# A two-layer diffusion-transformer step: the conditioning parts in another order, some of them placed at stage borders, and a first MLP group of eight tiles

## The chip, the cores and the metric

The kernel runs on one NeuronCore of a Trainium2 chip. The metric is the device time of one execution in microseconds (us); lower is better. The time before is the median of three runs.

## The reference, cut to what matters

Two streams of 128 tokens each (context and latent) with 2048 channels pass through two layers. Layer 0 mixes tokens with differential attention and a two-way RWKV-7 scan; layer 1 is a Conformer convolution module. A gated ConvFFN (the MLP) follows each of them. All is in float32.

```python
def adaln(cvec, w, b):                      # w_ada: (2 layers, 2048, 6*2048)
    return (silu(cvec) @ w + b)[:, None, :]

for l in range(2):
    sh1, sc1, g1, sh2, sc2, g2 = split(adaln(c, w_ada[l], b_ada[l]), 6)   # once for c, once for c_ctx
    h = rmsnorm(x, norm_g[l, 0]) * (1 + sc1) + sh1
    m = ab_mixer(h, ...) if l == 0 else conformer_conv(h, ...)
    x = x + g1 * m
    h = rmsnorm(x, norm_g[l, 1]) * (1 + sc2) + sh2
    x = x + g2 * conv_ffn(h, w_up[l], w_ffn_dw[l], w_down[l])
y = rmsnorm(x, final_norm_g)

def conformer_conv(h, ...):
    u = h @ w_pw1                           # 2048 -> 4096
    u = u[..., :2048] * sigmoid(u[..., 2048:])
    u = dwconv(u, w_dw) + b_dw              # 31 taps
    return silu(layernorm(u)) @ w_pw2

def conv_ffn(h, ...):                       # D_FF = 5504 = 43 tiles of 128
    u = dwconv(h @ w_up, w_ffn_dw)          # 3 taps
    gate, val = split(u, 2)
    return (silu(gate) * val) @ w_down
```

The twelve vectors `sh1 ... g2` of two layers are the conditioning. Each is a product of two vectors (`c` and `c_ctx`, through SiLU) with a 2048 x 2048 piece of `w_ada`, so 16.8 MB of weights are read for each of them and almost nothing is computed.

## The kernel before, in words

Activations lie with channels on the 128 partitions and 256 tokens (two streams of 128) on the free axis; 2048 channels are 16 tiles, counted by `kt`. Matrix products go through `gemm` (line 235). A plan is a list of groups; a group is a set of output tiles that accumulate in PSUM together. For each group `gemm` walks over all `kt`, and for each `kt` and each output tile TensorE issues three matmuls of 128x128 by 128x256: high part of the weight by high part of the activation (line 252), high by low (254), low by high (255). So a group of four tiles costs 12 matmuls in each `kt`, one of eight tiles 24. In the last group of some products (`tail=4`) the last four `kt` are issued tile by tile (lines 268 to 270), with an optional call `between()` ahead of them.

The weights come from HBM in pieces of 128 x 1024 floats (512 KB) into a tile `raw` (`emit_load`, line 180). ScalarE copies the high part to a slot of `wbt` (line 192) and VectorE, or GpSimd for the Conformer's products, subtracts for the low part (line 194). There are 7 buffers of `raw`, 4 slots of `wbt`, and the loads run some six sub-pieces ahead. All these loads, and those of `w_ada`, are issued by SyncE in one queue.

After each `kt`, `gemm` calls `pump(2)`, which advances the evacuation of the group before, and then `fill()`, a function that each stage sets for itself. The `fill` functions advance the conditioning by one step (`ada_step`). The conditioning is one Python generator (`ada_gen`) that goes through `ada_order`, a list of parts; a part is one vector's half, 8 tiles of 128 columns, except for the first two vectors, which are cut finer. A part is worked in one of two ways:

- `ada_pe`, on TensorE: for each `kt` one 512 KB load and 8 matmul records of 128x32 by 128x256 (line 431). With `batch` 1 a step is one `kt` and is loaded at the step; with `batch` 2 a step is two `kt` (16 records), and the two loads of the next step are issued one step ahead. A part is 16 `kt`.
- `ada_vec`, on VectorE, for the parts in `AS_VEC`: for each `kt` one load and two fused multiply-adds over 128x1024 (line 456), one for each of `c` and `c_ctx`; a step is one of them. At the end 16 matmul records (line 464) sum over the partitions. A part is 38 steps.

`ada_until(l, name)` runs the generator until that vector is there. What each stage needs is forced in this way: `g2` of layer 0 before the first down projection, `sh1` and `sc1` of layer 1 before the Conformer, and so on. The text order of the program is only a priority: a scheduler that knows the data dependences orders each engine's queue, and pulls work forward where an engine would idle. `high_priority(300)` lets a piece go ahead of 300 instructions.

The stages from the output projection on, and where the conditioning stood before:

1. `w_out` (`p_outs`), with one conditioning step per four `kt` (`fill_out`).
2. First MLP (`ffn(0, ...)`): up 22 tiles, down 22, up 21, down 21, in groups of four output tiles (two gate, two value) for the up products. `fill0`: a step per two `kt` after the 16th, until the first half of layer 1's `g1` is done.
3. Conformer: `p_p1` in nine groups whose sizes are in `sizes` (number of channel tiles; a group has twice as many output tiles, for the gate). The 31 taps of the convolution run on VectorE, one fused multiply-add per tap and channel tile (line 1655); for the last three groups 4, 14 and 16 of the taps go to TensorE (`n_pe`, line 1648). `fill1`: a step per four `kt` after the 16th, and more while the last taps are worked off. Then the layer norm's sums and broadcast (lines 1710 and 1732), then `p_p2` without a `fill`, then `ada_until(1, "sh2")`.
4. Second MLP (`ffn(1, ...)`), `fill2`: a step per two `kt` after the 16th, with the two halves of layer 1's `g2`, then the final norm.

Between two stages stands a border: the last residual (line 667), the sums of squares by TensorE (line 528, `rstd_tok`), a square root and a reciprocal, a broadcast by TensorE (line 543, `rstd_bcast`), and then the modulated, split activation `hbt`, which is made one `kt` after the other by `modulated` (lines 582, 585, 587), while the first group of the next product already consumes it.

## Time and profile before

| | |
|---|---|
| runs | 2729.94, 2709.16, 2708.67 us; median 2709.16 us |
| the profiled execution | 2707.69 us, its span 2705.6 us |
| mean granted TensorE clock | 0.977 |
| TensorE matmul busy | 2615.6 us, 97% of the span, 24347 instructions |
| VectorE busy | 2020.5 us, 75% |
| ScalarE busy | 1258.5 us, 47% |
| HBM | 226 GB/s over the span |

The profile is of one execution. The span runs from the first to the last instruction. Stretches are given in us from the start of the span. In the view of stretches a row gives, for each stretch, its length, the busy time of each engine with the number of its instructions in brackets, the granted TensorE clock, the mean busy share of the DMA engines and their rate. In the timeline a row gives start, duration, engine, line, operation, what it writes and reads, and how many were merged; idle time ahead of it stands in square brackets with what ended it.

### The profile page before, as it was taken

How to read it: one execution, taken by the hardware profiler on the slowest of the kernel's cores; microseconds unless marked ns; L12 is line 12 of the kernel's file. 1: busy time of each engine (PE TensorE's matmuls, PEld its weight loads, DVE VectorE, ACT ScalarE, POOL GpSimd, SP SyncE). 2: the span in 40 equal slices, each digit the busy share in tenths (PEclk: the TensorE clock that was granted, in tenths of full speed). 3: DMA queues.
4: the chain of work that ended last, by engine and by line, in shares of the span. 5: the costliest groups of instructions: out<-in, count | busy, mean ns of one | idle time of the engine just before them, and what ended most of it. 6: DMA issues, size and time to landing. Idle time of an engine off the chain costs nothing.

```text
span 2705.6 us, 60522 instructions
## 1 busy us (share of the span) xinstructions
PE 2615.6 (97%) x24347; PEld 2443.4 (90%) x24347; DVE 2020.5 (75%) x3468; ACT 1258.5 (47%) x2074; POOL 298.7 (11%) x313
## 2 busy tenths in 40 slices
PE   6999998999999999999999989999999999999998
PEld 5889996667898999999999989978889999999998
DVE  3457765767579998978999989996479985566655
ACT  3335654554345444434444454346344454355544
POOL 2000012011100000000000047653200000000000
PEclk8999999999799999999999989999999999999999
DMA  9997656655356887877878857865798876666653
GB/s 293 304 272 209 204 169 217 243 193 199 129 189 195 257 268 240 286 249 247 277 247 267 274 169 246 275 229 177 243 299 277 258 234 195 195 195 193 194 190 119
DMA packets 446969, 616.59 MB, mean 228 GB/s; under 512 B 33461, under 2 KB 317464, under 8 KB 446048
## 3 DMA queue, kind: packets, MB, share of 16 engines
q1 hardware_dynamic: 442288, 600.83, 70.2%
q0 software_dynamic: 3040, 6.57, 0.7%
q10 hardware_dynamic: 1360, 5.33, 0.5%
q8 instruction: 191, 3.13, 0.5%
q14 instruction: 90, 0.74, 0.1%
HBM read 604.75 MB, written 7.86 MB: 226 GB/s over the span
## 4 chain that ended last, share of the span: by engine, by line
PE 84%; DVE 7%; DMA 6%; ACT 1%; issue 1%; SPq 0%; POOL 0%; DVEq 0%; ACTq 0%; POOLq 0%
PE mm L255 22%; PE mm L252 22%; PE mm L254 22%; PE ada L431 4%; DVE cu L1655 3%; DMA raw<-in_w_ada 2%; DMA raw<-in_w_in 2%; PE mm L1087 1%; DVE wbt L194 1%; DMA raw<-in_w_up 1%; PE mm L304 1%; PE mm L306 1%; PE mm L305 1%; PE mm L1648 1%; PE mm L1120 1%
## 5 line engine op out<-in xcount | busy, mean ns | idle before, releaser
L192 ACT ACTIVATE wbt<-raw 128x1024 fp32r<-128x1024 f32 (+3 forms) x768 | 793.7, 1037 | 1035.4 <-PE mm L254 696.8
L252 PE MATMUL mm<-hbt,wbt 128*128 128x256 f32 x3888 | 1086.5, 282 | 6.0 <-ACT hbt L585 2.3
L254 PE MATMUL mm<-hbt,wbt 128*128 128x256 f32 x3888 | 1081.5, 280 | 2.7 <-DVE hbt L587 2.7
L194 DVE TENSOR_TENSOR wbt<-raw,wbt 128x1024 fp32r<-128x1024 f32 (+1 forms) x688 | 812.6, 1188 | 357.7 <-ACT wbt L192 345.5
L255 PE MATMUL mm<-hbt,wbt 128*128 128x256 f32 x3888 | 1064.2, 280 | 3.5 <-DVE wbt L194 3.3
L252 PEld LDWEIGHTS mm<-hbt,wbt 128*128 128x128 f32 x3888 | 733.3, 189 | 20.3 <-issue 9.2
L254 PEld LDWEIGHTS mm<-hbt,wbt 128*128 128x128 f32 x3888 | 734.0, 189 | 6.9 <-DVE hbt L587 4.7
L255 PEld LDWEIGHTS mm<-hbt,wbt 128*128 128x128 f32 x3888 | 723.2, 189 | 9.7 <-DVE wbt L194 4.7
L254 PE MATMUL mm<-u,wbt 128*128 128x256 f32 x1344 | 371.0, 278 | 0.0
L252 PE MATMUL mm<-u,wbt 128*128 128x256 f32 x1344 | 370.9, 278 | 0.0
L255 PE MATMUL mm<-u,wbt 128*128 128x256 f32 x1344 | 365.7, 278 | 0.0
L456 DVE SCALAR_TENSOR_TENSOR av<-raw,silu_c,av 128x1024 f32<-128x1024 f32 x270 | 337.2, 1278 | 29.6 <-DMA raw<-in_w_ada 29.5
L194 POOL TENSOR_TENSOR wbt<-raw,wbt 128x1024 fp32r<-128x1024 f32 x80 | 193.5, 2427 | 909.8 <-DMA raw<-in_w_pw 800.2
L252 PEld LDWEIGHTS mm<-u,wbt 128*128 128x128 f32 x1344 | 252.2, 188 | 0.4 <-issue 0.4
L254 PEld LDWEIGHTS mm<-u,wbt 128*128 128x128 f32 x1344 | 252.0, 188 | 0.4 <-issue 0.4
L255 PEld LDWEIGHTS mm<-u,wbt 128*128 128x128 f32 x1344 | 249.1, 188 | 0.4 <-issue 0.4
L431 PE MATMUL ada<-raw,silu_c 128*32 128x256 f32 (+2 forms) x2688 | 166.0, 337 | 31.3 <-DMA raw<-in_w_ada 15.6
L1655 DVE SCALAR_TENSOR_TENSOR cu<-mm,vec,cu 128x256 f32<-128x256 f32 x428 | 174.4, 470 | 2.2 <-ACT cu L1639 1.0
L1544 DVE SCALAR_TENSOR_TENSOR cv<-mm,vec,cv 128x254 f32<-128x254 f32 x344 | 147.3, 474 | 11.8 <-ACT cv L1539 11.8
L431 PEld LDWEIGHTS ada<-raw,silu_c 128*32 128x32 f32 x2688 | 70.3, 112 | 91.7 <-issue 26.2
L304 PE MATMUL mm<-hbt,wbt 128*128 128x256 f32 x304 | 91.7, 302 | 1.9 <-DVE qkv L311 1.0
L1539 ACT ACTIVATE cv<-mm,vec 128x256 f32<-128x256 f32 x172 | 72.0, 474 | 45.9 <-PE mm L255 45.8
(449 smaller groups left out, 2889.6 us busy)
## 6 DMA issues: line engine op xcount, KB each, us to landing
raw<-in_w_ada SPq DMA_DIRECT2D x384, 512.0 KB, 5.3
raw<-in_w_up SPq DMA_DIRECT2D x688, 256.0 KB, 4.2
raw<-in_w_down SPq DMA_DIRECT2D x168, 512.0 KB, 5.0
raw<-in_w_pw SPq DMA_DIRECT2D x128, 256.0 KB, 4.3
raw<-in_w_in SPq DMA_DIRECT2D x128, 192.0 KB, 6.1
raw<-in_w_in SPq DMA_DIRECT2D x48, 512.0 KB, 3.9
raw<-in_w_out SPq DMA_DIRECT2D x32, 512.0 KB, 4.0
raw<-in_w_pw SPq DMA_DIRECT2D x32, 512.0 KB, 4.7
```

The lines of the kernel that those rows point to most:

```text
L192: act.activation(w[:, 0, 0:na * n], v, AF.Copy)
L194: pl.lo(pl.count).tensor_tensor(out=w[:, 1, 0:na * n], in0=v, in1=w[:, 0, 0:na * n].bitcast(F32), op=ALU.subtract)
L252: pe.matmul(ps, lhsT=hi, rhs=r[:, 0:TT], start=(ki == 0 and (nl > 0 or j % 2 == 0)), stop=False, skip_group_check=True)
L254: pe.matmul(ps, lhsT=hi, rhs=r[:, TT:2 * TT], start=False, stop=False, skip_group_check=True)
L255: pe.matmul(ps, lhsT=lo, rhs=r[:, 0:TT], start=False, stop=(ki == nk - 1), skip_group_check=True)
L304: pe.matmul(ps, lhsT=hi, rhs=r[:, 0:TT], start=(i == 0), stop=False, skip_group_check=True)
L305: pe.matmul(ps, lhsT=hi, rhs=r[:, TT:2 * TT], start=False, stop=False, skip_group_check=True)
L431: pe.matmul(ps[32 * j:32 * j + 32, 0:nb * 32], lhsT=silu_c[:, kt, :], rhs=rv[:, j], start=(kt == 0), stop=(kt == KT - 1))
L456: dve.scalar_tensor_tensor(out=av[:, s], in0=raw, scalar=sc, in1=av[:, s], op0=ALU.mult, op1=ALU.add)
L1539: act.activation(o, ps, AF.Copy, scale=w(1, ct))
L1544: dve.scalar_tensor_tensor(out=o[:, :, a_], in0=v2(ps)[:, :, b_], scalar=w(k, ct), in1=o[:, :, a_], op0=ALU.mult, op1=ALU.add)
L1655: dve.scalar_tensor_tensor(out=o, in0=pads[a](k), scalar=V("w_dw", k * KT + ct), in1=o, op0=ALU.mult, op1=ALU.add)
```

## The change

- `ada_order`: layer 1's `sc2` and `sh2` alternate by halves; the rest keeps its order.
- `AS_VEC`: now layer 1's `sc1`, `sh1`, `g1` (both halves each) and the second half of both `g2`: 8 parts, one fewer than before. The first halves of both `g2` and all of layer 1's `sc2` and `sh2`, 6 parts, are in the new list `AHEAD`: on TensorE, with two `kt` in a step and the loads two steps ahead (`depth` 2). The other TensorE parts keep `batch` 1.
- `ada_first(...)`, as `between` ahead of the tail of `w_out`, of the first MLP and of `p_p2`: finish what the stage owes, then take two steps, which are the four loads of the next part. After each of these products `ada_step(2)`, and `modulated` gets `gap=ada_step`, called after the sums and again after the broadcast. Two more pairs of steps stand around the layer norm's broadcast in the Conformer.
- `fill_out` only until `sh2` of layer 0 is done; `fill0` and `fill2` from the first `kt` on, `fill0` until all of layer 1's `g1` is done; `fill1` a step per two `kt` up to the 8th and then one per eight, now also in `p_p2`; none while the Conformer's last taps are worked off.
- The first group of each MLP's up product has eight output tiles in place of four, and the Conformer's sizes are six groups of two, then 1, 2, 1, in place of 1, seven of two, 1. The list `n_pe` and the index of the tiles whose mean is corrected stay the same.

```diff
--- before.py
+++ after.py
@@ -394,12 +394,15 @@
     K0 = [sum(KS[:i]) for i in range(len(KS))]
     NP0 = len(KS)
     ada_order = [(0, nm, i, NP0, K0[i], KS[i]) for i in range(NP0) for nm in ("sc1", "sh1")]
-    ada_order += [(l, nm, i, 2, 8 * i, 8) for l in range(2) for nm in ("sc1", "sh1", "g1", "sc2", "sh2", "g2")
-                  for i in range(2) if l or nm not in ("sc1", "sh1")]
-    AS_VEC = [(l, nm, i) for l, nm in ((0, "g2"), (1, "sc1"), (1, "sh1"), (1, "g2")) for i in range(2)] + [(1, "g1", 0)]
+    ada_order += [(l, nm, i, 2, 8 * i, 8) for l, nm, i in
+                  [(0, nm, i) for nm in ("g1", "sc2", "sh2", "g2") for i in range(2)] +
+                  [(1, nm, i) for nm in ("sc1", "sh1", "g1") for i in range(2)] +
+                  [(1, nm, i) for i in range(2) for nm in ("sc2", "sh2")] + [(1, "g2", i) for i in range(2)]]
+    AS_VEC = [(l, nm, i) for l, nm in ((1, "sc1"), (1, "sh1"), (1, "g1")) for i in range(2)] + [(0, "g2", 1), (1, "g2", 1)]
+    AHEAD = [(0, "g2", 0), (1, "sc2", 0), (1, "sh2", 0), (1, "sc2", 1), (1, "sh2", 1), (1, "g2", 0)]
     ada_done = set()
 
-    def ada_pe(l, nm, b0, nb, batch):
+    def ada_pe(l, nm, b0, nb, batch, depth):
 
 
         ps = psa.tile([P, 256], F32, tag="ada", name="ada")
@@ -416,11 +419,11 @@
         k0s = list(range(0, KT, na))
         steps = [k0s[i:i + batch] for i in range(0, len(k0s), batch)]
         ahead = []
-        if batch > 1:
-            ahead.append([load(k0) for k0 in steps[0]])
+        for st_ in steps[0:depth]:
+            ahead.append([load(k0) for k0 in st_])
             yield
         for i in range(len(steps)):
-            nxt = i + len(ahead)
+            nxt = i + depth
             if nxt < len(steps):
                 ahead.append([load(k0) for k0 in steps[nxt]])
             for raw, k0 in ahead.pop(0):
@@ -476,7 +479,7 @@
             if (l, nm, part) in AS_VEC:
                 tr = yield from ada_vec(l, nm, b0, nb)
             else:
-                tr = yield from ada_pe(l, nm, b0, nb, 2 if l else 1)
+                tr = yield from ada_pe(l, nm, b0, nb, *((2, 2) if (l, nm, part) in AHEAD else (1, 0)))
             bias = V(f"b_ada{l}", si * KT + b0, nb)
             av = adaT[:, l * 6 + si, 2 * b0:2 * (b0 + nb)].rearrange("p (b s) -> p b s", s=2)
             dve.tensor_tensor(out=av, in0=tr, in1=bias.unsqueeze(2).to_broadcast([P, nb, 2]), op=ALU.add)
@@ -565,12 +568,19 @@
         rhs.upto = upto
         return rhs
 
-    def modulated(x, acc, l, ni, known=False):
+    def modulated(x, acc, l, ni, known=False, gap=lambda: None):
         sh = "sh1" if ni == 0 else "sh2"
 
         def gen(hb):
-            with tc.high_priority(0):
-                rs = acc if known else rstd_bcast(rstd_tok(acc))
+            if known:
+                rs = acc
+            else:
+                with tc.high_priority(0):
+                    sd = rstd_tok(acc)
+                gap()
+                with tc.high_priority(0):
+                    rs = rstd_bcast(sd)
+                gap()
             for kt in range(KT):
                 t = nrm_[0].tile([P, TT], F32, tag="ht", name="ht", bufs=3)
                 for st in range(3):
@@ -624,7 +634,7 @@
     full = [grp([512 * q], 512, [0, P, 2 * P, 3 * P], q=q) for q in range(4)]
     p_outs = [Plan(view_for(A["w_out"][0]), full, list(range(8 * i, 8 * i + 8))) for i in range(2)]
     g_p1 = []
-    sizes = [1] + [2] * 7 + [1]
+    sizes = [2] * 6 + [1, 2, 1]
     for q, n in enumerate(sizes):
         c = sum(sizes[:q])
         g_p1.append(grp([P * c, D + P * c], P * n, [P * j for j in range(2 * n)], q=q, c=c, n_=n))
@@ -637,7 +647,7 @@
             gs = []
             i = a
             while i < b:
-                n = min(2, b - i)
+                n = 4 if i == 0 else min(2, b - i)
                 gs.append(grp([i * P, DFF + i * P], n * P, [P * j for j in range(2 * n)], i=i, n_=n))
                 i += n
             return Plan(view_for(A["w_up"][l]), gs, list(range(KT)))
@@ -1519,10 +1529,19 @@
 
             def fill_out():
                 cnt[0] += 1
-                if cnt[0] % 4 == 0:
+                if cnt[0] % 2 == 0 and (0, "sh2") not in ada_done:
                     ada_step()
-            gemm(p_outs[1], lambda kt: hm[1][:, kt - 8], residual(0, "g1", acc), fill_out, tail=4)
+
+            def ada_first(*seg):
+
+                def between():
+                    ada_until(*seg)
+                    ada_step(2)
+                return between
+            gemm(p_outs[1], lambda kt: hm[1][:, kt - 8], residual(0, "g1", acc), fill_out, tail=4,
+                 between=ada_first(0, "sh2"))
             drain()
+            ada_step(2)
 
 
             def ffn(l, pls, acc, fill, hb, between=None):
@@ -1574,19 +1593,20 @@
                     drain()
 
             ada_until(0, "sh2")
-            hb = modulated(x, acc, 0, 1)
+            hb = modulated(x, acc, 0, 1, gap=ada_step)
             acc = new_acc()
             cnt = [0]
 
             def fill0():
                 cnt[0] += 1
-                if cnt[0] % 2 == 0 and cnt[0] > 16 and (1, "g1", 0) not in ada_done:
+                if cnt[0] % 2 == 0 and (1, "g1") not in ada_done:
                     ada_step()
-            ffn(0, p_f0, acc, fill0, hb)
+            ffn(0, p_f0, acc, fill0, hb, ada_first(1, "g1"))
+            ada_step(2)
 
 
             ada_until(1, "sh1")
-            hb = modulated(x, acc, 1, 0)
+            hb = modulated(x, acc, 1, 0, gap=ada_step)
             with scoped("cv", 1) as cvp, scoped("cvt", 2) as cvt:
                 HW = CW // 2
                 u = cvp.tile([P, KT, TT], F32, name="cu")
@@ -1679,7 +1699,7 @@
 
                 def fill1():
                     cnt[0] += 1
-                    if cnt[0] % 4 == 0 and (1, "sh2") not in ada_done and cnt[0] > 16:
+                    if (cnt[0] % 2 == 0 if cnt[0] <= 8 else cnt[0] % 8 == 0) and (1, "sh2") not in ada_done:
                         ada_step()
 
                 cnt[0] = 0
@@ -1689,8 +1709,6 @@
                         for g_ in list(pending):
                             if next(g_, "end") == "end":
                                 pending.remove(g_)
-                    if (1, "sh2") not in ada_done:
-                        ada_step()
                 while stats:
                     step_stats()
                 warm = nrm_[0].tile([P, 1], F32, tag="warm", name="warm")
@@ -1710,6 +1728,7 @@
                             pe.matmul(ps[:, c0 + 2 * s:c0 + 2 * s + 2], lhsT=src[:, s * T:(s + 1) * T], rhs=ones[:, 0:2],
                                       start=first, stop=False, skip_group_check=True)
                             first = False
+                ada_step(2)
                 mv = nrm_[0].tile([P, 8], F32, tag="mv", name="mv")
                 dve.tensor_scalar(out=mv, in0=ps[:, 0:8], scalar1=1.0 / D, scalar2=None, op0=ALU.mult)
                 va = nrm_[0].tile([P, 8], F32, tag="va", name="va")
@@ -1730,6 +1749,7 @@
                                           op0=ALU.mult)
                 pbc = bank()
                 pe.matmul(pbc, lhsT=ones, rhs=dg.rearrange("p a t -> p (a t)"), start=True, stop=True)
+                ada_step(2)
                 hc = new_hb()
                 for ct in range(KT):
                     t = cvt.tile([P, TT], F32, tag="cg", name="cg")
@@ -1740,16 +1760,16 @@
                     split(hc[:, ct], sl, pool if ct % 2 else dve)
                 acc = new_acc()
                 ada_until(1, "g1")
-                gemm(p_p2, lambda kt: hc[:, kt], residual(1, "g1", acc), tail=4)
+                gemm(p_p2, lambda kt: hc[:, kt], residual(1, "g1", acc), fill1, tail=4, between=ada_first(1, "sh2"))
                 drain()
-            ada_until(1, "sh2")
-            hb = modulated(x, acc, 1, 1)
+            ada_step(2)
+            hb = modulated(x, acc, 1, 1, gap=ada_step)
             acc = new_acc()
             cnt[0] = 0
 
             def fill2():
                 cnt[0] += 1
-                if cnt[0] % 2 == 0 and cnt[0] > 16:
+                if cnt[0] % 2 == 0:
                     ada_step()
             ot, orow = [None], [None]
 
```

## The prediction

> **What bounds the kernel now.** I read the page's first part, then its chain.
>
> ```profile
> PE 2615.6 (97%) x24347; PEld 2443.4 (90%) x24347; DVE 2020.5 (75%) x3468; ACT 1258.5 (47%) x2074; POOL 298.7 (11%) x313
> PE 84%; DVE 7%; DMA 6%; ACT 1%; issue 1%; SPq 0%; POOL 0%; DVEq 0%; ACTq 0%; POOLq 0%
> ```
>
> TensorE is the bound: 97% busy and 84% of the chain. So a change can win in two places: where TensorE idles, or in what each matmul costs. Next comes the view of stretches, cut at the borders from the end of `w_out` on (length; PE, PEld, DVE, ACT, POOL busy and counts; granted clock; DMA share; GB/s), then the same for line 431 alone.
>
> ```profile
> 822.00:836.00 14.00, 8.94 (x41) 7.66 (x39) 11.56 (x38) 7.27 (x19) 0.00 (x0) 0.63 0.37 111
> 836.00:1576.00 740.00, 736.59 (x6267) 729.23 (x6266) 674.93 (x856) 343.61 (x468) 2.56 (x2) 1.00 0.82 259
> 1576.00:1610.00 34.00, 25.68 (x176) 23.29 (x176) 28.47 (x72) 20.64 (x50) 17.27 (x8) 0.80 0.29 94
> 1610.00:1762.00 152.00, 151.47 (x1367) 141.21 (x1366) 144.45 (x341) 59.27 (x72) 113.90 (x49) 1.00 0.80 254
> 1762.00:1800.00 38.00, 35.23 (x262) 30.42 (x263) 35.68 (x95) 15.65 (x27) 21.47 (x9) 0.91 0.71 221
> 1800.00:1848.00 48.00, 43.46 (x302) 28.95 (x301) 31.31 (x74) 27.06 (x69) 15.82 (x15) 0.98 0.68 239
> 1848.00:1941.00 93.00, 92.15 (x768) 92.16 (x768) 56.38 (x97) 51.56 (x79) 40.70 (x22) 0.98 0.55 170
> 1941.00:1986.00 45.00, 36.39 (x325) 20.00 (x325) 18.39 (x62) 12.92 (x33) 0.00 (x0) 0.73 0.96 342
> ```
>
> ```profile
> 1610.00:1762.00 152.00, 14.99 (x224) 1.00 0.80 254
> 1762.00:1800.00 38.00, 4.44 (x48) 0.91 0.71 221
> 1800.00:1848.00 48.00, 11.03 (x128) 0.98 0.68 239
> 1941.00:1986.00 45.00, 21.15 (x240) 0.73 0.96 342
> ```
>
> The worst place is the border ahead of the second MLP, 1941 to 1986. Of its 325 matmuls 240 are conditioning (15 steps of 16) and ten belong to the norm; 75 are left for the product, 8.8 us at the 117.6 ns found below. So 36.2 of 45 us are lost to it. The chain says to whom:
>
> ```profile
> 1941.23 3.20 PE ada L431 x56
> 1944.93 9.91 DMA raw<-in_w_ada
> ...
> 1972.03 7.26 DMA raw<-in_w_up
> ```
>
> 30 loads of 0.524 MB are 15.7 MB, 46 us at the 342 GB/s of that row: the border waits for conditioning weights, and then for MLP weights queued behind them. For comparison, the border ahead of the first MLP has no conditioning: 14 us, 41 matmuls less ten, 31 x 117.6 ns = 3.6, so 10.4 us lost. Its timeline shows how:
>
> ```profile
> 822.02 0.28 PE L270 MATMUL mm<-hm,wbt 128*128 128x256 f32 x1
> 824.89 0.35 PE L528 MATMUL mm<-ones,acc 128*128 128x2 f32 x2 [2.60 <-DVE acc L517]
> ...
> 827.52 1.22 PE L543 MATMUL mm<-dg,ones 128*128 128x256 f32 x2 [1.00 <-ACT dg L540]
> 829.91 0.79 PE L252 MATMUL mm<-hbt,wbt 128*128 128x256 f32 x2 [1.17 <-ACT hbt L585]
> ...
> 831.60 0.41 PE L252 MATMUL mm<-hbt,wbt 128*128 128x256 f32 x1
> 831.81 0.41 PE L254 MATMUL mm<-hbt,wbt 128*128 128x256 f32 x1
> ```
>
> Three holes of 2.60, 1.00 and 1.17 us, then matmuls 0.21 us apart: the array runs at half clock until about 835.4.
>
> One more thing sets the time, and it is not in any wait. I asked for stretches between two breaks of the matmul stream by conditioning (TensorE alone). There are nine of over 50 us; the first and the last:
>
> ```profile
> 928.00:1037.00 109.00, 109.00 (x927) 1.00 0.83 259
> 2210.00:2680.00 470.00, 470.00 (x4150) 1.00 0.61 189
> ```
>
> No idle time, clock 1.00 in all; yet 117.6 and 113.3 ns per matmul, and the other seven are like the first. The pace changed right at the last conditioning matmul:
>
> ```profile
> 2205.94 0.28 PE L255 MATMUL mm<-hbt,wbt 128*128 128x256 f32 x1
> 2206.15 0.64 PE L464 MATMUL ada<-av,sel 128*32 128x256 f32 x8
> 2206.72 0.39 PE L255 MATMUL mm<-hbt,wbt 128*128 128x256 f32 x1
> 2207.00:2686.00 479.00, 479.00 (x4229) 479.00 (x4229) 286.33 (x395) 225.26 (x294) 0.00 (x0) 1.00 0.60 186
> ```
>
> I read this as two steady rhythms of loading weights and multiplying: a break decides which one follows, and it holds until the next break. The fast one saves 4229 x 117.6 ns - 479 = **18.3 us**. One of the three runs of before is 21 us longer than the other two; losing the fast rhythm would do about that.
>
> **The change, part by part.** A step of two `kt` inside a running product costs:
>
> ```profile
> 1654.53 0.28 PE L255 MATMUL mm<-hbt,wbt 128*128 128x256 f32 x1
> 1654.74 1.07 PE L431 MATMUL ada<-raw,silu_c 128*32 128x256 f32 x16
> 1655.74 0.39 PE L252 MATMUL mm<-hbt,wbt 128*128 128x256 f32 x1
> 1655.96 0.28 PE L254 MATMUL mm<-hbt,wbt 128*128 128x256 f32 x1
> ```
>
> From 1654.53 to 1655.74 are 1.21 us where 0.12 was due, and the next start is 0.22 on where 0.12 was due: 1.2 us. A part is eight steps. Since stage 1, six parts or 48 steps take the place of five parts or 40.
>
> *Border ahead of the second MLP.* The burst goes; the border becomes like the first MLP's, with four steps in its holes. 4.8 us of steps fit 4.77 us of holes, so they are free and may keep half the slow matmuls (24 at 0.21) fast: 10.4 - 1.2 = 9.2 lost instead of 36.2, **-27**. Half of `sh2` may still be late, but it is needed only from `kt` 8, after 8 x 24 x 117.6 ns = 22.6 us of the eight-tile group.
>
> *Border ahead of the first MLP.* Four steps of `g2` in the holes, free; -1.2 for the clock. Eight tiles double the work in each `kt` while `hbt` is being made, and end most of this:
>
> ```profile
> PE mm L255 <- DVE wbt L194: 3.3, 4, 1.4
> ```
>
> Those are TensorE's waits within 836 to 1576. I take 1.8 of the 3.3: **-3**. The eight-tile evacuation (26 yields at two per `kt`) ends inside the next group; it holds four of seven banks, the next group takes two. I cost it at nothing; without that cover the third group would wait for a bank.
>
> *Steps now exposed.* Four in the first MLP, four in the second. In `p_p2`, which had none, `fill1` is called 60 times: seven calls, of which four are matmul steps, the others loads or ends of parts; and six calls remain ahead of its tail, five of them matmul steps. 17 x 1.2 = 20.4; against it the second MLP loses one VectorE part, whose 16 records on line 464 cost 1.1: **+19.3**.
>
> *Conformer, first product and its border.* 15 steps instead of 25, so -12 if TensorE alone were the bound. But VectorE is busy 144.45 of 152 us with the taps:
>
> ```profile
> L1655 DVE SCALAR_TENSOR_TENSOR cu<-mm,vec,cu 128x256 f32<-128x256 f32 x428 | 174.4, 470 | 2.2 <-ACT cu L1639 1.0
> L456 DVE SCALAR_TENSOR_TENSOR av<-raw,silu_c,av 128x1024 f32<-128x1024 f32 x270 | 337.2, 1278 | 29.6 <-DMA raw<-in_w_ada 29.5
> ```
>
> The first group has two channel tiles instead of one: 192 matmuls (22.6 us) and four steps, instead of 96, so the taps start some 10 us later; about 6 stay, as VectorE idled 7.5 us in 1610 to 1762. The last taps lose their eight steps (11 us by the row of 1800 to 1848, VectorE's idle time there 16.7): -7. Half clock ahead of it: -3. Against that stands a debt: `fill0` is called 504 times, 252 steps, and the first MLP owes 5 + 7 x 38 = 271. The 19 left over, 14 of them multiply-adds of 1.28 us, come ahead of the tail and so ahead of the border's `hbt` on VectorE. The scheduler pulls some forward, VectorE's idle time takes some: +6 of 17.9. Four taps return to VectorE (1.6). Sum about **+3**, bounds -12 and +15.
>
> *Conformer's norm.* Four steps in two holes; warmer clock: **-1**. *Buffers:* two steps ahead hold four of the seven `raw` buffers through the Conformer; three of them turning over in 5.3 us after the issue plus a copy feed one per 2.8 us, so nothing; -0 to +6.
>
> ```profile
> raw<-in_w_ada SPq DMA_DIRECT2D x384, 512.0 KB, 5.3
> ```
>
> *Rhythm.* The last break now falls some 78 us earlier in the second MLP (86 calls of `fill2`, 16 of them at 2.8 us and 70 at 1.4, are 144 us; before it was 221). Which rhythm follows is drawn anew. One of nine long stretches was fast, and none behind a line-431 step. So I take it as lost: **+18**. New draws in the first MLP: -1.
>
> Sum: -27 - 3 + 19 + 3 - 1 + 18 - 1 = **+8 us**. The profiled execution took 2707.7 us (span 2705.6 and 2.1 around it), 1.5 below the median; the sum is set on the median 2709.2, so 2717.
>
> The Trainium skill ("TensorE: Matmul & The Clock Gate", Part 1: The HAM clock gate) says that the array drops to half clock after an idle window of about 3.4 us and comes back after as much work; the rows at 831.60 agree. By its rule alone the filled holes, none over 3.4 us, would keep all 24 matmuls fast, 2.3 us per border where I took 1.2.
>
> **The rivals.**
>
> *The fast rhythm is kept.* It may belong to the second MLP once conditioning is done, not to chance. For it: 470 us without a lapse, and two of three runs alike. Against it: the stage 836 to 1576 and `p_p2`, which has no conditioning at all, never had it. It gives 2717 - 18 and a further 78 x 3.6% = 3: 2696. [...]
>
> *Slower: the debt of the first MLP is paid at its border.* All 14 multiply-adds go ahead of `hbt` on VectorE: 17.9 us instead of my 6, and the Conformer's taps have no room to give it back. For it: VectorE busy 674.93 of 740 us in that MLP, where the parts need about what they get. Against it: conditioning matmuls at 1575.97 that by the count of steps belong to the Conformer had been pulled ahead. 2717 + 12 = 2729. It decides from about eight multiply-adds left over at the tail.
>
> *The spreading does not hold.* The scheduler, or a lack of `raw` buffers, lets the Conformer's parts fall behind, and half the burst stays at the second MLP: +13, 2730. For it: in the row of 1941 the queue, not TensorE, was the limit.
>
> **How the numbers follow.** The forecast 0.5, the kept rhythm 0.25, the debt 0.15, the failed spreading 0.1. The forecast's own range by its unknown terms is 2702 to 2732. To hold eight in ten the range reaches down to the kept rhythm, less a few us, and up past the two slower cases by little: 2692 to 2733. One per cent, 27 us, is about what a measurement of this kernel can tell from no change. Faster than that (below 2682) needs the kept rhythm and the Conformer at its good end: 0.15. Slower (above 2736) needs the lost rhythm and a rival in full: 0.1. Within: 0.75.
>
> **What would show it.** In the profile after: the border ahead of the second MLP under 16 us with under 10 lost, and no line-431 burst there; gaps of 1.2 us in `p_p2`; at the end of the first MLP line-456 work on VectorE between the tail and the first `hbt`; and in the last 400 us of the second MLP the count of matmuls per stretch, 117.6 or 113.3 ns each. I am wrong if the rhythm is fast there or in the first MLP, or if `p_p1` follows TensorE rather than VectorE.

## The result, and the profile after

The changed kernel took 2746.57 us (median of four runs, 2742.53 to 2754.72), the kernel before 2708.91 (four runs, 2704.42 to 2729.94): about one per cent longer. The ratio on record is 1.0104, with a 95% interval of 1.0058 to 1.0149; the two medians alone would give 1.0139. I had forecast 2717, and 2733 as the upper end: some 30 us too low. The profiled execution took 2754.72 us, span 2752.7, 47.1 more than before's 2705.6. In the new line numbers the conditioning matmul is 434 (431 before), the VectorE multiply-add 459 (456), its sum on TensorE 467 (464), the border's sums 531 (528), the taps 1675 (1655), the mean correction 1697 (1677), the norm's sums 1728 (1710).

From the first and last start of each product's matmuls in the two traces I cut both spans into the same stretches (us):

| stretch | before | after | difference | forecast |
|---|---|---|---|---|
| start to the output projection, the mixer in it | 715.4 | 727.9 | +12.5 | 0 |
| output projection, border, first MLP | 860.3 | 857.7 | -2.6 | some +1 |
| border ahead of the Conformer, first product, norm | 273.1 | 294.1 | +21.0 | +2 |
| Conformer's second product without tail | 86.6 | 97.2 | +10.6 | +5 |
| its tail | 5.5 | 12.8 | +7.3 | +6 |
| border ahead of the second MLP and that MLP's first product | 287.2 | 267.6 | -19.6 | -22 |
| rest of the second MLP, end | 477.5 | 495.4 | +17.9 | +17 |

(The +17 are the 18 of the rhythm less 1.1 for one part fewer on VectorE.) The last two rows came near their forecast. The border ahead of the second MLP, in the timeline of TensorE after (the last product matmul ahead of it started at 1989.72):

```profile
1989.84 0.28 PE L531 MATMUL mm<-ones,acc 128*128 128x2 f32 x2
1990.05 1.50 PE L434 MATMUL ada<-raw,silu_c 128*32 128x256 f32 x24
...
1995.28 1.08 PE L434 MATMUL ada<-raw,silu_c 128*32 128x256 f32 x8 [1.27 <-DMA raw<-in_w_ada]
1996.29 1.22 PE L252 MATMUL mm<-hbt,wbt 128*128 128x256 f32 x4
```

6.6 us to the first product matmul where before had 16.6, with steps in the holes and no burst of 15. And the rest of the second MLP, in the view of stretches (length, busy PE with its matmuls in brackets, PEld, DVE, ACT, POOL, granted clock, DMA share, GB/s):

```profile
2150.00:2730.00 580.00, 580.00 (x4927) 580.00 (x4926) 338.37 (x465) 267.10 (x352) 0.00 (x0) 1.00 0.59 181
```

580 us / 4927 = 117.7 ns: the slow rhythm, where before ran at 113.3.

The loss that I did not see lies in the Conformer. First its border, in the timelines of VectorE and TensorE; the first MLP's last product matmul started at 1585.57:

```profile
1588.58 1.28 DVE L459 SCALAR_TENSOR_TENSOR av<-raw,silu_c,av 128x1024 f32<-128x1024 f32 x1
1589.77 0.42 DVE L520 TENSOR_TENSOR acc<-acc,sq 128x256 f32<-128x256 f32 x1
1590.11 2.47 DVE L459 SCALAR_TENSOR_TENSOR av<-raw,silu_c,av 128x1024 f32<-128x1024 f32 x2
1592.50 0.42 DVE L520 TENSOR_TENSOR acc<-acc,sq 128x256 f32<-128x256 f32 x1
1592.84 3.67 DVE L459 SCALAR_TENSOR_TENSOR av<-raw,silu_c,av 128x1024 f32<-128x1024 f32 x3
```

```profile
1593.07 0.56 PE L531 MATMUL mm<-ones,acc 128*128 128x2 f32 x2 [7.22 <-DVE acc L520]
```

The debt of the first MLP stands between the last residuals, ahead of the additions of the squares (line 520) that the border's sums wait 7.22 us for: seven multiply-adds start behind the last product matmul, where before has none.

The second piece needs one term. The layer norm does not wait for all 16 channel tiles: as soon as the taps of tiles 0 to 12 are done, TensorE takes their mean (line 1696), ScalarE copies it (1697), and then 13 subtractions, squares and sums follow, tile by tile. I call this the chain of statistics, and its start the mean correction. Here is the end of the taps, from all engines' timeline, and TensorE's waits from 1852 to 1876 (us in total, times, longest):

```profile
1848.81 0.42 DVE L1693 TENSOR_TENSOR acc<-acc,cu 128x256 f32<-128x256 f32 x1
...
1853.55 0.59 PE L1696 MATMUL mm<-acc,m0w 128*128 128x256 f32 x2
...
1854.18 0.38 ACT L1697 ACTIVATE m<-mm 128x256 f32<-128x256 f32 x1 [1.33 <-PE mm L1696]
...
1854.64 5.92 POOL L1625 TENSOR_TENSOR cu<-cu,m 128x256 f32<-128x256 f32 x7 [29.06 <-ACT m L1697]
...
1867.90 0.42 DVE L1633 TENSOR_TENSOR accq<-accq,csq 128x256 f32<-128x256 f32 x1 [0.90 <-POOL accq L1633]
1868.37 0.92 PEld L1728 LDWEIGHTS mm<-ones,csq 128*128 128x128 f32 x4 [11.38 <-ACT csq L1722]
```

```profile
PE mm L1728 <- ACT csq L1722: 11.3, 1, 11.3
PE mm L1751 <- ACT dg L1746: 1.8, 1, 1.8
```

and the mean correction before:

```profile
1809.71 0.37 ACT L1677 ACTIVATE m<-mm 128x256 f32<-128x256 f32 x1
```

When the taps ran is told by the view of one line, before and after (count, shortest, median and longest ns, first and last start):

```profile
L1655 DVE SCALAR_TENSOR_TENSOR cu<-mm,vec,cu x428: 429/471/486, 1612.8 to 1829.7; 128x256 f32<-128x256 f32 x143
```

```profile
L1675 DVE SCALAR_TENSOR_TENSOR cu<-mm,vec,cu x432: 401/476/486, 1643.5 to 1851.6; 128x256 f32<-128x256 f32 x144
```

Before, the mean correction came at 1809.71, 20 us ahead of the last tap (1829.7), and its 13 subtractions, squares and sums ran beside the remaining taps. After, it comes at 1854.18, 2.6 us behind the last tap (1851.6). The sum of tile 12, its last input, was made at 1848.81; the mean's matmul followed at 1853.55, behind taps of later tiles in TensorE's queue. Before, the way from that last sum (1800.94) to the correction was longer, 8.8 us, but it lay far ahead of the last tap. Nothing is left to hide the chain: TensorE waits 11.3 us, and the clock falls with it, in the view of stretches:

```profile
1860.00:1886.00 26.00, 13.75 (x56) 12.05 (x57) 11.53 (x34) 14.98 (x31) 6.31 (x9) 0.54 0.00 1
```

0.54 of the clock (the column ahead of the DMA share), where 26 us around the same step before had 0.87:

```profile
1838.00:1864.00 26.00, 22.12 (x155) 20.43 (x155) 18.30 (x44) 17.78 (x35) 8.66 (x7) 0.87 0.27 85
```

The Trainium skill ("TensorE: Matmul & The Clock Gate", Part 1: The HAM clock gate) has the array at half clock after an idle window of some 3.4 us until one such window is busy; the trace agrees: after the 11.3-us wait the norm's few matmuls do not fill a window, and half clock stays for 23.9 us.

The +12.5 of the first row is one more half clock, in the mixer, whose instructions are those of before in the same order on TensorE:

```profile
585.00:613.00 28.00, 28.00 (x173) 19.39 (x171) 10.20 (x26) 10.73 (x21) 1.14 (x4) 0.51 0.31 99
```

It took 305.3 us here and 295.5 in a second trace of the same kernel, 290.9 and 294.9 in two of before. Two traces of kernels with before's order of the parts had such a record too, and took 304.4 and 301.4. It is a draw of the execution, not of the change, and accounts for some 10 of the 47 us of the profiled runs.

### The profile page after: what moved, and what is told of

The parts are those of the page before. It is cut to its first block, busy times and chain, and to the rows that moved or that the text cites. A ratio compares the mean times of both kernels' runs of the same rounds, so it can differ in the third digit from the quotient of the medians.

```text
span 2752.7 us, 60617 instructions
## 1 busy us (share of the span) xinstructions
PE 2649.3 (96%) x24451; PEld 2467.8 (90%) x24451; DVE 1982.1 (72%) x3439; ACT 1262.5 (46%) x2069; POOL 298.8 (11%) x313
## 4 chain that ended last, share of the span: by engine, by line
PE 85%; DMA 6%; DVE 5%; ACT 1%; POOL 1%; issue 1%; SPq 1%; ACTq 0%; POOLq 0%; DVEq 0%
PE mm L252 22%; PE mm L255 22%; PE mm L254 22%; PE ada L434 4%; DMA raw<-in_w_ada 2%; DMA raw<-in_w_in 2%; DMA raw<-in_w_pw 2%; PE mm L1097 2%; DVE cu L1675 2%; PE mm L304 1%; DVE wbt L194 1%; PE mm L1668 1%; PE mm L306 1%; PE mm L305 1%; POOL wbt L194 1%
## 5 line engine op out<-in xcount | busy, mean ns | idle before, releaser
L459 DVE SCALAR_TENSOR_TENSOR av<-raw,silu_c,av 128x1024 f32<-128x1024 f32 x240 | 300.6, 1279 | 13.4 <-DMA raw<-in_w_ada 13.3
L434 PE MATMUL ada<-raw,silu_c 128*32 128x256 f32 (+2 forms) x2816 | 180.6, 345 | 38.6 <-DMA raw<-in_w_ada 32.6
L434 PEld LDWEIGHTS ada<-raw,silu_c 128*32 128x32 f32 x2816 | 76.0, 115 | 100.9 <-issue 33.7
```

The lines of the kernel that those rows point to most:

```text
L434: pe.matmul(ps[32 * j:32 * j + 32, 0:nb * 32], lhsT=silu_c[:, kt, :], rhs=rv[:, j], start=(kt == 0), stop=(kt == KT - 1))
L459: dve.scalar_tensor_tensor(out=av[:, s], in0=raw, scalar=sc, in1=av[:, s], op0=ALU.mult, op1=ALU.add)
```

## The experiments

Two sums serve below: F, from the end of the first MLP to the first matmul of the second MLP's first down product (the border, the Conformer, the next border, the up product; 652.4 before, 671.7 after), and R, from there to the last product matmul of the second MLP (464.0 and 481.9). By the table my forecast for F was -9; it was +19.3, and that is the miss.

**Group sizes.** In the changed kernel, and then the reverse in the kernel before:

```
- sizes = [2] * 6 + [1, 2, 1]
+ sizes = [1] + [2] * 7 + [1]
```

> The changed kernel with the old groups in the Conformer's first product (1, seven times 2, 1 channel tiles). From the first matmul of that product to the end of the second product's tail the changed kernel took 387.7 us where before took 355.1. Theory A (the group sizes: a first group of two tiles starts the taps late, and channel tile 12, alone in its group, ends so late that the chain of statistics stands exposed, 11.3 us of idle TensorE ahead of the norm's sums): this stretch shrinks by 15 to 22 us, the idle ahead of the sums to under 3 us, the total to about 2727 us. Theory B (the debt of the first MLP: its multiply-adds and its loads stand ahead of the product's weights and of the taps): the stretch shrinks by 5 us at most, total 2742 to 2747. In both the stretch at the end of the second MLP is a new draw of TensorE's rhythm: 18 us less if it comes out fast, to be set apart by its matmul period.

> The kernel before with only the new group sizes in the Conformer's first product (six times 2, then 1, 2, 1). Theory A (sizes cost): the stretch from its first matmul to the end of the second product, 355.1 us before, grows by 12 to 20 us, with idle TensorE ahead of the norm's sums, total 2721 to 2729 if the rhythm at the end stays fast. Theory B (the debt costs, not the sizes): within 4 us of 2709. My prediction had put this part at +6 for the late start and +1.6 for four taps, less 7 for the steps, so about 2714 by it.

Old sizes in the changed kernel: 2743.61 us (1.0105 of before, 1.0049 to 1.0161), F 661.6; the first tap comes 46.6 us behind the first MLP's end instead of 57.9, the correction 11 us ahead of the last tap, and TensorE's idle ahead of the sums is 4.6 us. The Conformer went from 387.7 to 372.8: 14.9 us less, just under the 15 to 22 of theory A. The total did not follow: A had put it at about 2727. New sizes in the kernel before: 2727.54 us (1.0041, 1.0007 to 1.0074), with the Conformer at 343.2, *shorter* than before's 355.1. That is not theory A as I put it. Its total is longer all the same: in its trace R is 481.9 and the mixer has the half clock. Of the 12 us some 5 are TensorE's rhythm (some 1200 matmuls of the two products ran at 113.3 ns); a later run of the same sizes (below) had 351.2, and a second trace of before 350.5. So the sizes alone cost the Conformer nothing; they cost it some 15 us only beside the other edits.

**The debt.**

```
- if cnt[0] % 2 == 0 and (1, "g1") not in ada_done:
+ if (cnt[0] % 2 == 0 or cnt[0] % 26 == 13) and (1, "g1") not in ada_done:
```

> The changed kernel with 19 more conditioning steps spread over the first MLP (one more in every 26 calls), so that nothing is left over for its tail. Theory B (the debt): the border ahead of the Conformer goes from 16.5 back to some 10 us, the first tap comes about 10 us sooner, weights are loaded sooner, and the total falls by 12 to 18 us to 2730. Theory A (the sizes): only the border's 6.4 us come back, total about 2740. If VectorE cannot take more multiply-adds within the first MLP (it is busy 675 of 740 us there), the steps pile up behind it anyway and nothing changes.

2740.29 us (1.0111, 1.0074 to 1.0148). The border fell from 16.5 to 9.1 us, the first tap came at 47.6 instead of 57.9: the debt's price at the first tap is 10.3 us, theory B's figure. But the total fell by 6 us, not by B's 12 to 18: the first MLP grew by 5.1, and F fell by 5.7 only (9.8 against the repetition below): with the taps 10 us earlier the correction was still behind the last of them (257.1 and 254.6 us behind the first MLP's end), and TensorE waited 5.3 and 6.8 us there. So debt and statistics are two causes.

**The eight-tile groups.**

```
- n = 4 if i == 0 else min(2, b - i)
+ n = min(2, b - i)
```

> The changed kernel with the first group of both MLPs back at four tiles (two by two) instead of eight. The first MLP gets back the 3.3 us of waits for VectorE that the eight tiles took away, and the second MLP's start, which took 267.4 us from the border to the end of its first product, some 3 to 8 more: total 2750 to 2756, if the eight tiles are a gain at all. If the four banks that the group holds, or its long evacuation, cost something that I priced at nothing, it is 2740 or less. The debt and the sizes stay as they are, so the Conformer's stretch should stay at 385 to 390 us by either theory.

2738.1 us (1.0075, 1.0033 to 1.0118), 8 us below the changed kernel, where a gain of the eight tiles would have shown as 2750 to 2756. The first MLP took 745.7 (742.2 with eight tiles, of which 2.9 are a fast stretch of some 650 matmuls, and 741.9 to 745.5 in six other traces of kernels with eight and the same steps), the stretch behind the next border 267.4 (267.6). Whatever the eight tiles bring is below what these traces can tell. What they cost can be seen: the two small groups call `fill0` 16 times more than the one large group, and so pay eight of the 19 owed steps. In this run no multiply-add is left behind the last product matmul, the border takes 11.9 us instead of 16.5, the first tap comes at 49.7 instead of 57.9, and F is 663.1. So the run changes the debt too, and its 8 us at the first tap are the debt's, brought about by the large group.

**The statistics.** `C0` is the number of channel tiles whose mean is taken early, 13 in both kernels and 12 in this run:

```
- C0 = g_p1[-2]['c']
+ C0 = g_p1[-3]['c']
```

> The changed kernel with the mean correction taken from channel tiles 0 to 11 instead of 0 to 12, so that the chain of statistics no longer waits for tile 12, whose taps run side by side with those of tiles 13 to 15. In the changed kernel the correction came 268.6 us after the first MLP's end, 2.6 us behind the last tap, and the norm's last sum 21.8 us behind that tap. Theory C (the chain of statistics is exposed because tile 12 ends with the last taps): the correction comes at about +243, the last sum 9 to 12 us behind the last tap, the half clock ahead of the second product shrinks from 23.9 us, and the stretch from the product's first matmul to the end of the second product's tail falls from 387.7 to about 375; total 2732 to 2736. Theory D (the taps alone set the end, and the chain behind them is a matter of the norm itself): the last sum stays 18 to 22 us behind the last tap, total 2743 to 2747.

> The changed kernel once more, for a second trace of it and for times on the chip of the other runs. If the stretches repeat, the Conformer takes 386 to 389 us again, the border ahead of it 16 to 17, and the last 480 us of the second MLP run at 117.8 ns per matmul. The mixer took 305.3 us in the first trace with a half-clock record of 27.3 us at 585, and 291 to 294 us in three other kernels without such a record: if that is chance, it is about 292 now and the span 2739 to 2742; if it belongs to the change, it is 305 again.

The repetition: 2749.8 us (1.0124, 1.0071 to 1.0177), Conformer 387.5, F 675.8, R 481.9, mixer 295.5. The stretches repeat. With the mean taken of 12 tiles in place of 13, one group earlier, the correction comes 236.6 us behind the first MLP's end, and the norm's last sum 8.5 us behind the last tap instead of 21.8 (as much in the repetition); of TensorE's 11.3-us wait nothing is left:

```profile
PE mm L252 <- ACT hbt L550: 2.0, 1, 2.0
PE mm L1751 <- ACT dg L1746: 1.8, 1, 1.8
```

(its waits from 1845 to 1870). The Conformer takes 376.6, 11 us less, as theory C had it. The median is 2743.27 (1.0109, 1.0055 to 1.0163), higher than forecast; its four runs spread from 2732.9 to 2755.9, so the gain rests on the traces.

**The spreading.** Once without it, once with more of it inside the product (a flag tells `fill1` which product it serves):

```
- gemm(p_p2, ..., residual(1, "g1", acc), fill1, tail=4, between=ada_first(1, "sh2"))
+ gemm(p_p2, ..., residual(1, "g1", acc), tail=4)
+ ada_until(1, "sh2")
```

> The changed kernel with no conditioning step inside the Conformer's second product and none ahead of its tail: what is left of sc2 and sh2 is taken at the border ahead of the second MLP again, as in the kernel before. My sum had spreading gain 27 us at that border and cost 10.8 us of steps in and around the product. The traces showed -19.6 at the border and the product behind it, and +17.9 in the product and its tail. If the spreading pays as I forecast, this kernel is 10 to 16 us slower, 2757 to 2762; if it only moves the time, as the traces suggest, it is within 4 us, 2743 to 2750, with the product back at 87 us, its tail at 5.5, and the border with the next product back at 285 to 290 us instead of 267.

```
- cnt[0] % 8 == 0
+ cnt[0] % (4 if (1, "g1") in ada_done and on_p2[0] else 8) == 0
```

> The changed kernel with one conditioning step at every fourth call inside the Conformer's second product instead of every eighth, so that 15 calls take place in it and little is left for its tail. If the dear part is the handful of steps ahead of the tail, each waiting for its own load (7.3 us more than before in the tail), the tail falls from 12.8 to 6 or 7 us, the product grows by about 4 us, and the total is 2 to 5 us lower. If the loads cannot keep up with steps at every fourth call (two loads of 0.5 MB in 5.6 us of product, on top of its own weights), the waits move into the product and the total stays within 2 us.

With the burst back at the border: 2746.45 us (1.0115, 1.007 to 1.016), the product 88.0, the tail 5.5, border and next product 279.9, F 671.0: the same as with the spreading. The spreading of the change moves 12 to 16 us from one side of the tail to the other, and gains none. The reason is in the tail of the changed kernel, TensorE's timeline without the product matmuls:

```profile
1971.33 1.93 PE L434 MATMUL ada<-raw,silu_c 128*32 128x256 f32 x32
1976.35 0.64 PE L434 MATMUL ada<-raw,silu_c 128*32 128x256 f32 x8 [3.08 <-DMA raw<-in_w_ada]
1980.14 0.64 PE L434 MATMUL ada<-raw,silu_c 128*32 128x256 f32 x8 [1.78 <-DMA raw<-in_w_ada]
```

The steps forced ahead of the tail outrun the loads two steps ahead and wait for them. With a step at every fourth call the tail is 5.5 us, the product no longer (97.6), and F 665.7: 6 to 10 us less. The median of 2751.15 (1.0141, 1.0079 to 1.0203) does not show it; its four runs lie between 2739 and 2768.

**The rhythm.** A load and four useless matmuls behind the last conditioning part, and before once more:

```
+ raw = rawp.tile(...); sp.dma_start(out=raw, in_=A["w_ada"][1, 0:P, 0:1024])
+ for _ in range(8): yield
+ ...                           # ps: a PSUM tile, rv: raw seen as four blocks
+ for j in range(4):
+     pe.matmul(ps[32*j:32*j+32, 0:256], lhsT=silu_c[:, 0, :], rhs=rv[:, j], start=True, stop=True)
```

> The changed kernel with one more load and four more conditioning matmuls (8 records, 0.7 us) of no use a few calls behind the last conditioning part of the second MLP, so that the last break of TensorE's stream is another one. In eight profiles of kernels with the changed order of conditioning the last break was always one of line 467 (6 or 8 records), the second product matmul behind it came 229 or 230 ns after the first, and the rest ran at 117.8 ns; in the kernel before it was a break of line 464 with 222 ns behind it, and the rest ran at 113.3. Theory R (the way in which the stream resumes behind the last break sets the pace until the next one; with 221 to 223 ns it can be fast, with 224 and more hardly ever): breaks of eight records on line 434 were followed by the fast pace 14 times in 33, so here the last 4900 matmuls may run at 113.3 ns, 20 us less, in some of the runs; with an interval of 224 ns or more in the profile they do not. Theory S (the fast pace belongs to the old order of the second MLP): 117.8 ns in all runs, 2743 to 2750.

> The kernel before once more, for a second trace. Its times fall into groups near 2706, 2716, 2725 and 2733 us. If two things are drawn anew in each execution, the pace of the last 480 us (18 us apart) and a stretch of half clock in the mixer of some 27 us (10 to 13 us apart), the trace shows which of the two this one has: with the slow pace its last stretch takes 482 us instead of 464, with the half clock its mixer 304 instead of 291. If it is all as in the first trace, this look tells nothing on it.

With the extra break 2727.7 us (1.0037, 1.0006 to 1.0068), 19 to 22 us below the changed kernel, with more work. In the timeline of TensorE, the last break of the changed kernel, of this one, and of before's second trace:

```profile
2144.00 0.64 PE L467 MATMUL ada<-av,sel 128*32 128x256 f32 x8
2144.57 0.39 PE L255 MATMUL mm<-hbt,wbt 128*128 128x256 f32 x1
2144.80 0.28 PE L252 MATMUL mm<-hbt,wbt 128*128 128x256 f32 x1
```

```profile
2162.09 0.64 PE L503 MATMUL ada<-raw,silu_c 128*32 128x256 f32 x8
2162.66 0.39 PE L252 MATMUL mm<-hbt,wbt 128*128 128x256 f32 x1
2162.89 0.28 PE L254 MATMUL mm<-hbt,wbt 128*128 128x256 f32 x1
```

```profile
2199.87 0.64 PE L464 MATMUL ada<-av,sel 128*32 128x256 f32 x8
2200.44 0.39 PE L255 MATMUL mm<-hbt,wbt 128*128 128x256 f32 x1
2200.66 0.28 PE L252 MATMUL mm<-hbt,wbt 128*128 128x256 f32 x1
```

and the stretches behind the last two, in the view of stretches:

```profile
2170.00:2690.00 520.00, 520.00 (x4591) 520.00 (x4589) 314.92 (x434) 248.72 (x326) 0.00 (x0) 1.00 0.60 190
```

```profile
2210.00:2690.00 480.00, 480.00 (x4078) 480.00 (x4077) 277.13 (x379) 217.82 (x281) 0.00 (x0) 1.00 0.58 182
```

520 us / 4591 is 113.3 ns, the fast pace; 480 / 4078 is 117.7, in the *kernel before*: its second trace (2720.15 us, R 481.9) has lost the rhythm that its first one had. The interval from the first to the second product matmul behind the break, to the nanosecond, was 229 in the changed kernel, 222 with the extra break, 222 in before's first trace and 224 in its second.

**Repairs together.** First the three (extra steps in the first MLP, `C0`, every fourth call), then more beside the extra break:

> The changed kernel with the three repairs that the runs point to together: 19 more steps in the first MLP (no debt), the mean correction from tiles 0 to 11, one step at every fourth call in the Conformer's second product. From the stretches: debt about -10 from the first MLP's end to the first tap and +4 in the first MLP, the statistics -11, the steps ahead of the tail -7, so 2742 to 2750 less 24: 2718 to 2726 at the slow pace of the second MLP, and the stretch from the first MLP's end to the end of the Conformer's tail at 370 us instead of 404 (365 in the kernel before). If the three overlap (the taps' start given back by later taps, as without the debt the statistics came no sooner in the first trial), only 10 to 15 us come back: 2730 to 2736.

2726.51 us (1.0031, 1.0009 to 1.0054) at the slow pace: R 481.9, F 652.5, before's own. In F they add up against the first trace of the changed kernel (5.7, 7.2 and 6.0 from the single runs; measured 19.2), and fall short against its second (9.8, 11.3 and 10.1; measured 23.3). But the stretch to the tail's end is at 386.6, not 370: with the statistics beside them the taps take 216 us instead of 208.

> The kernel before with the new group sizes in the Conformer's first product and the useless extra break (one load, 8 records) behind the last conditioning part of the second MLP. The new sizes alone made the Conformer 11.9 us shorter in the kernel before (343.2 for 355.1), and the extra break gave the changed kernel the fast pace at the end in most runs. Together: 2690 to 2697 us if the extra break is followed by the fast pace, 2708 to 2715 if by the slow one. If the sizes' gain was a matter of one run's pace (the second product ran fast in that one), the Conformer is at 347 to 351 here.

> The changed kernel with the three repairs (no debt, correction from tiles 0 to 11, a step at every fourth call in the second product) and the extra break. The three repairs alone gave 2726.5 us with the slow pace at the end. Theory R (the way in which the stream resumes sets the pace): 2706 to 2710 if the second matmul behind the extra break comes at 222 ns, 2724 to 2728 if at 224 or more.

> The changed kernel with the old group sizes in the Conformer's first product, no debt, a step at every fourth call in the second product, and the extra break. From the first MLP's end to the end of the Conformer's tail the three repairs took 386.6 us, the kernel before 365.2 and 360.5. The old sizes with the debt took 390.6; less 9 for the debt and 6 for the tail this should be about 375. If TensorE's fewer steps in the first product are what hurts (the last groups' products are ready too early, their taps run side by side with those of tile 12, and the statistics wait), the correction comes about as late as with the old sizes and the debt, some 11 us ahead of the last tap, and 375 holds; under 365 would say that the debt was the whole of it.

> The changed kernel with the conditioning steps of the Conformer put back to where the kernel before takes them (none in the first 16 calls, then at every fourth, and the rest while the last taps run), with no debt and with the extra break; new sizes, new order of parts, eight-tile groups and steps at the borders stay. Theory E (the wide spreading over the Conformer is what hurts: steps in the first group delay the first tap, too few later let the product run ahead of VectorE so that the last four tiles' taps run side by side and the statistics wait, and the steps in the second product and ahead of its tail lie bare): the first tap comes at +43 instead of +58 us behind the first MLP's end, the correction 12 us or more ahead of the last tap, the last sum within 11 us behind it, the second product takes 84 to 88 and its tail 5.5 us; from the first MLP's end to the end of that tail 350 to 360 us instead of 404. Total 2675 to 2685 with the fast pace at the end, 18 more with the slow one. If the order of parts or the loads two steps ahead are what hurts, 375 or more of these 404 us stay.

| kernel | median | of before, interval | F | R | interval behind the extra break |
|---|---|---|---|---|---|
| before, new sizes, extra break | 2704.44 | 0.9957 (0.9932 to 0.9981) | 650.5 | 465.3 | 223 ns |
| three repairs, extra break | 2704.24 | 0.9949 (0.9921 to 0.9978) | 644.8 | 464.0 | 222 ns |
| old sizes, no debt, every fourth call, extra break | 2704.40 | 0.9969 (0.9942 to 0.9996) | 643.3 | 464.0 | 223 ns |
| before's steps in the first product, no debt, extra break | 2703.48 | 0.9966 (0.9937 to 0.9994) | 643.3 | 464.0 | 223 ns |

All four have the fast pace and end within 1 us of each other. They are some 40 us below the changed kernel and 0.3 to 0.5% below before. But before's own 31 times beside them run from 2702 to 2731, 13 of them from 2702 to 2711, and its F was 652.4 and 647.8. So most of the gain over before appears to be that the extra break makes the fast pace regular, in before itself (the first row) as well.

For theory E, which I had put on the last, the answer is no: the first tap came at 50.8, not 43, and from the first MLP's end to the tail's end it took 383 us, not 350 to 360. With all steps of `sc2` and `sh2` in the first product TensorE had no gap between 1834 and 1866, and the norm's last sum came 18 us behind the last tap. One part of E held: with the steps put back into the first product the correction came 14.3 us ahead of the last tap, where the run without the debt had it 2.5 us behind. So, with the new sizes, it was the lack of steps in that product that let it run ahead of VectorE. Three different placements give the same F: the steps have to lie somewhere, and once nobody waits bare for them, it matters little where.

**A break behind every part.**

```
+ if (l, nm, part) in AS_VEC:   # 3 yields later, rhs: the part's last load
+     ...
+     for j in range(4): pe.matmul(ps[32*j:32*j+32, 0:256], lhsT=silu_c[:, 0, :], rhs=rv[:, j], ...)
```

> The changed kernel with the three repairs, and a useless break of 8 records (silu_c against the part's last load, no load of its own) some calls behind each of the eight conditioning parts made on VectorE, seven of them in the first MLP. So far the stretches of 720 to 860 matmuls between the parts of the first MLP ran at 117.8 ns each time, behind breaks of line 467 in their many sizes. Theory R (what counts is how the stream resumes; behind an extra break of 8 records it resumed at 222 or 223 ns and ran at 113.3 in five profiles of five): six or seven stretches of the first MLP run at 113.3 ns, 3.2 to 3.8 us less each, less 0.7 for each break: the first MLP takes 725 to 732 us instead of 743 to 747, the total 2686 to 2694 beside 2704 with the one extra break. Theory S (the pace is settled by the stage, and only the last stretch can be fast): the first MLP stays at 743 to 750, total 2704 to 2710.

2708.43 us (0.9984, 0.9955 to 1.0013); the first MLP took 747.9. Theory R fell in its strong form: only one long stretch of that MLP went fast. But the intervals say which. The one with 223 ns, and the first with 224:

```profile
968.63 0.39 PE L252 MATMUL mm<-hbt,wbt 128*128 128x256 f32 x1
968.85 0.28 PE L254 MATMUL mm<-hbt,wbt 128*128 128x256 f32 x1
...
1068.62 0.39 PE L254 MATMUL mm<-hbt,wbt 128*128 128x256 f32 x1
1068.84 0.28 PE L255 MATMUL mm<-hbt,wbt 128*128 128x256 f32 x1
```

```profile
970.00:1030.00 60.00, 60.00 (x532) 60.00 (x531) 58.21 (x72) 29.61 (x43) 0.00 (x0) 1.00 0.87 278
1070.00:1150.00 80.00, 80.00 (x682) 80.00 (x681) 76.40 (x92) 33.08 (x39) 0.00 (x0) 1.00 0.85 285
```

60 / 532 is 112.8 ns, 80 / 682 is 117.3. Of the seven breaks of this kind inside a product, those with 222 and 223 were followed by the fast pace (two of two), those with 224 and 225 by the slow one (five of five).

## Why the prediction was wrong, point by point

- **The failed step is "Conformer, first product and its border"**, +3 with an upper bound of 15, together with the norm's -1. It measured +21.0, and between the second traces of both kernels (268.7 and 296.4) +27.7. Its parts, from the first traces:
  - The late start by the group sizes, forecast 6, was 6.4 with the new sizes in before.
  - The debt, forecast 6, was 10.3, between my figure and the 17.9 of the rival: seven multiply-adds stood behind the last product matmul, not all 14, and the taps did not give the time back. Eight of the 19 owed steps came from the eight-tile group, which my count of 504 calls contained and my sum did not price.
  - Without the debt the first tap was still 4.2 behind that of before with the new sizes (47.6 against 43.4). The steps in the first group are not the reason: with none of them there (the run on theory E) it came at 50.8. In both of these runs eleven conditioning loads in a row stand in SyncE's queue around the first MLP's end, ahead of nearly all of the product's loads, where before with the new sizes has a single one; no run separates this, so the cause of the 4.2 stays open.
  - From the first to the last tap 216.9 us became 208.1, 8.8 less, forecast 7 less 1.6; before's second trace has 210.7, so this gain is within what a repetition moves. So far +12, inside the bounds.
  - The term that was not there at all is the chain of statistics: +8.4 us between the last tap and the last sum. I had priced the taps, and not asked when tile 12 is done. With the product ahead of VectorE (its last matmul came 32 us ahead of the last tap, 16 before), the last four tiles' taps are all ready and VectorE's queue takes them in turn, so tile 12 ends with the last instead of ahead of them. That the queue runs like this is read from its order. That it is the exposed chain which costs is shown by the run with 12 tiles, 11 us; that the fewer steps let the product run ahead, by the run on theory E.
- **Exposed steps** around the second product: forecast 9 x 1.2 = 10.8, measured 17.9. The count was near, 128 records or eight steps, the price was not: in the tail the steps waited for their loads, 3.08 and 1.78 us, which a step at every fourth call took away, and 3.4 us of half clock stood there. "The others are loads" of my count of seven calls was read as harmless; these loads were too few.
- **Border ahead of the second MLP**: -27 forecast, 4.8 of steps in that MLP's product to be set against it: -22, measured -19.6. Right. But with the second product's +17.9 nothing is left, as the run with the burst back shows: spreading was a wash.
- **Border ahead of the first MLP, eight tiles**: -3 forecast, not to be told from zero. The four steps were not quite free: the first product matmul came 9.2 us behind the last of `w_out`, 7.9 before. But 834 to 848 ran at a clock of 1.00 (0.88 over the same stretch of the second trace), where before's 822 to 836 had 0.63: the filled holes kept more of the clock than the half that I took. The length of a hole alone does not tell this, as before's holes of 2.60, 1.00 and 1.17 us were none over 3.4 us either, the length in the rule that the prediction draws on, and the array fell to half clock there.
- **The rhythm**, +18 forecast, +17.9 measured. Right in size, in part by luck: the trace of before that I started from had the fast pace, and the second trace of before did not. A break does decide, as I had read it. But the 18 us are a draw in before; in the changed kernel they were lost each time: 229 or 230 ns behind the last break in all nine traces without an extra one.
- **What would show me wrong** named a first product that follows TensorE instead of VectorE, not the order of the taps on VectorE; the sign that mattered, the correction behind the last tap, was not on the list.

## What to carry to other kernels

Ask of every chain that is hidden behind a long loop when its last input is finished, not only how long it is: an edit that lets one engine run ahead can make ready work interleave, and the input that everything waits for comes last. Work that is spread over a stage costs its own time plus the wait for its loads; a few steps forced at one place outrun a prefetch that was sized for even spacing. And before a difference of one per cent is explained, take a second trace of both kernels: here the kernel before alone ranged from 2698 to 2741 us, with two draws in it.

## What was not expected of the hardware

- Two steady paces of the same fp32r matmuls of 256 columns at full clock, 113.3 and 117.8 ns; which one follows goes with how the stream resumes. In the 18 traces of this study I took all stretches of 100 product matmuls and more from the output projection on, and the interval between the first two behind the break or wait that opened them: with 224 to 230 ns none of 213 was fast, with 222 or 223 ns 26 of 42, with less 4 of 47. So a short interval is needed for the fast pace here and does not suffice. What fixes that interval to a few nanoseconds stays open. The Trainium skill ("TensorE: Matmul & The Clock Gate", Back-to-back issue gap) gives N/2.4 + 2.5 ns as the warm gap of a single matmul by itself, by which I estimate 109 ns for 256 columns, and for streams of weight load and matmul it has measured spacings at 128 and 512 columns alone, and no second pace; none of these stretches ran at 109.
- A break of eight useless records gave the fast pace in the second MLP in all six traces that had one at its end, and 20 us; the same break in the first MLP did so in one of six stretches.
- The mixer dropped to half clock for 20 to 27 us in 3 of the 18 traces, with the same instructions, and took 301 to 305 us instead of 288 to 296. Why is open.
